# Turning cached keys: loads in 32-by-32 blocks and VectorE's block transpose in place of TensorE transposes

## Chip, cores, metric

The kernel runs on one core of a Trainium2 chip. The metric is the device time of one execution in microseconds (us); lower is better. One core has TensorE (PE: matrix products and transposes), VectorE (DVE), ScalarE (ACT), GpSimd (POOL), the SyncE queue (SP) from which this kernel issues all its DMAs, and 16 DMA engines. Each engine works through its own instructions in the order in which the compiled program has them.

## What is computed

One step of a two-layer encoder trunk for two groups of tokens: a new prompt of 512 tokens, and 8 running streams of 16 tokens each, with 256 cached rows per stream. Both groups share the weights and most of the work runs on all 640 rows at once. Cut to what matters here:

```python
for i in range(2):
    h = rmsnorm(x, g_mix[i])
    x = x + (fox_mixer(h, fox_cache) if i == 0 else mla_mixer(h, mla_cache))
    x = x + cross_attn(rmsnorm(x, g_cross[i]), mem_k[i], mem_v[i])
    x = x + swiglu(rmsnorm(x, g_ffn[i]))

# fox_mixer: 16 heads of 64; running streams see 256 cached keys and 16 new ones
s = einsum('bqhd,bkhd->bhqk', q, k_all) * FOX_SCALE + decay_bias
# cross_attn: 4 heads of 256 over 256 memory rows
s = einsum('bqhd,bkhd->bhqk', h @ w_q, mem_k) * X_SCALE
o = einsum('bhqk,bkhd->bqhd', softmax(s), mem_v) @ w_o
```

TensorE contracts over the partition axis. In `q . k` that axis is the head dimension, while the cached and memory keys lie in memory as rows of one token each. So every key tile has to be turned, from token-by-channel to channel-by-token, before its scores can be made.

## The kernel before

The program runs five kinds of stages: the FoX mixer (`fox_phase`), cross attention of layer 0 (`cross_phase`), feed-forward, the MLA mixer, cross attention of layer 1, feed-forward. Big products take weights in units of 128x1024 (`split_unit`): a DMA into one of two `raw` buffers, a rounded copy `whi` on ACT (L144), and the rest `wlo` by a subtraction on DVE (L145), with three buffers each. A product (`gemm`) is three passes over these parts, gathered in PSUM. Attention is written as lists of small steps, and `merge` spreads two or three lists evenly side by side, so that projections for the next heads stand between the steps of attention. The program's order on each engine follows from these lists; waits are on buffers and on data.

Keys are turned in three places.

- **FoX, running streams** (`sample_list` in `fox_phase`): 8 head pairs, each with two batches of 4 streams. `load` brings 128 channels of 1024 cached rows into `kr` (one buffer, 512 KB, L631), `vr` with the values, and `keys(0)`, `keys(1)` turn half of it each: four 128x128 transposes on TensorE into a PSUM tile (L641), then one copy to `KT`, on DVE for the first half (L645) and on ACT for the second (L647). That makes 32 steps.
- **Cross attention, running streams** (`sample_list` in `cross_phase`): per layer 2 head pairs x 2 batches x 2 heads x 4 streams. `keys` issues the DMA for one stream and head (256 KB, L886, ring `kr` of four buffers, shared with others), four transposes (L890), one copy (DVE L894 or ACT L896, by turns). 64 steps over both layers. `scores(0)` needs the first four of a list, `scores(1)` the other four.
- **Cross attention, prompt** (`prompt_list`): per layer 4 heads; keys and values of the prompt's memory come from DRAM (`kvd`, L827), four transposes (L835), then a split in two parts. 8 steps.

In each layer's cross attention the lists are run in four merges: the first two have the running streams, the prompt and a query projection (`q_list`) side by side, the last two have output projections in place of the query projection. `q_list` loads its 256 weight columns as two units of 128 columns with all 1024 rows, the second of them in the middle of the list:

```python
for half in range(2):
    for dt in range(2):
        if half == 0:
            L.append(lambda dt=dt: load(dt))
        L += gemm(... ws_ops(d[dt], slice(0, P), nx.T, ...), HALF, ..., parts=3)
```

Of the kernel before, what the change touches and what calls it, by code (L numbers as in the profile page):

```python
# [18 lines left out]
P = 128  # L19
# [61 lines left out]
def fox_mla_kernel(ctx: ExitStack, tc: tile.TileContext, I, O):  # L81
# [105 lines left out]
    def gemm(ops, n, done, parts=1):  # L187
        """One PSUM accumulation as a list of steps; ops() is asked for when the first step runs."""
# [15 lines left out]
    def merge(*lists):  # L204
        """Emits lists of steps side by side, each spread evenly over the whole."""
        steps = [((i + 0.5) / len(l), n, i) for n, l in enumerate(lists) for i in range(len(l))]
        for _, n, i in sorted(steps):
            lists[n][i]()
# [36 lines left out]
    class Act:  # L245
        """A transposed activation in two tiles of four row blocks each."""
# [36 lines left out]
    def out_norm(out_tile, g_row, cls=None):  # L283
        """Runs the last output projection of a phase tile by tile, each tile's norm behind it."""
# [42 lines left out]
    # ---------------------------------------------------------------- memory keys and values  # L327
    kvd = [drp.tile([2, NMEM, D], F32, name=f"kvd{l}") for l in range(2)]

    def mem_list(l, pool):  # L330
        """K and V of the prompt's memory, to the outputs and to DRAM for the cross attention."""
# [39 lines left out]
    # ---------------------------------------------------------------- FOX  # L371
    def fox_phase():
        w_in = I["w_fox_in"][0]
        w_out = I["w_fox_out"][0]
        ck = I["cache_fox_k"][0].rearrange("b (tt t) h d -> t (b tt) (h d)", t=P)
# [5 lines left out]
        with ExitStack() as st:  # L381
# [242 lines left out]
            def sample_list(pr):  # L624
# [4 lines left out]
                def load(bq):  # L629
                    d["kr"] = fp.tile([P, 8, P], F32, tag="kr", name="kr", bufs=1)  # L630
                    S.dma_start(d["kr"], ck[:, 8 * bq:8 * bq + 8, pr * P:(pr + 1) * P])  # L631
# [6 lines left out]
                def keys(b2):  # L638
                    pt = psum_t()
                    for i in range(4):  # L640
                        T.transpose(out=pt[:, i * P:(i + 1) * P], in_=d["kr"][:, 4 * b2 + i, :], identity=ident)  # L641
                    src = pt[:, :].rearrange("p (b t) -> p b t", t=PAST)
                    dst = d["KT"][:, 2 * b2:2 * b2 + 2, 0:PAST]
                    if b2 == 0:
                        V.tensor_copy(dst, src)  # L645
                    else:
                        A.copy(dst, src)  # L647
# [124 lines left out]
    # ---------------------------------------------------------------- cross attention  # L772
    def cross_phase(l, nx, rest):
        w_q, w_o = I["w_x_q"][l], I["w_x_o"][l]
        mk = I["cache_mem_k"][l].rearrange("b (m p) h d -> p (b m) (h d)", p=P)
        mv = I["cache_mem_v"][l].rearrange("b (m p) h d -> p (b m) (h d)", p=P)
        with tc.tile_pool(name=f"x{l}", bufs=2, reuse_waits="tile") as xp:
# [5 lines left out]
            def q_list(h):  # L783
# [4 lines left out]
                def load(dt):  # L788
                    if dt == 0:
                        qs_[h] = [xp.tile([P, 2, NP], F32R, tag=f"qT{i}", name=f"qT{i}", bufs=2) for i in range(2)]  # L790
                    c0 = h * XD + dt * P
                    d[dt] = load_w([(0, P, w_q[:, c0:c0 + P])], per=8)
# [11 lines left out]
                for half in range(2):  # L804
                    for dt in range(2):
                        if half == 0:
                            L.append(lambda dt=dt: load(dt))
                        L += gemm(lambda dt=dt, half=half: ws_ops(d[dt], slice(0, P), nx.T,
                                                                  slice(half * HALF, (half + 1) * HALF), KD),
                                  HALF, lambda ps, dt=dt, half=half: done(ps, dt, half), parts=3)  # L810
                return L
# [8 lines left out]
            def prompt_list(h):  # L820
                d = {}

                def load():
                    d["kv"] = []
                    for i in range(2):
                        r = xp.tile([P, 2, XD], F32, tag="kr", name="kr", bufs=4)
                        S.dma_start(r, kvd[l][i].rearrange("(t p) n -> p t n", p=P)[:, :, h * XD:(h + 1) * XD])  # L827
                        d["kv"].append(r)

                def keys():  # L830
                    d["kT"] = [xp.tile([P, 2, NMEM], F32R, tag=f"kT{i}", name=f"kT{i}", bufs=1) for i in range(2)]
                    pt = psum_t()
                    for dt in range(2):
                        for mt in range(2):
                            T.transpose(out=pt[:, dt * NMEM + mt * P:dt * NMEM + (mt + 1) * P],  # L835
                                        in_=d["kv"][0][:, mt, dt * P:(dt + 1) * P], identity=ident)
                    evac_split(d["kT"][0], d["kT"][1], pt.rearrange("p (d m) -> p d m", m=NMEM))
                    d["v"] = [xp.tile([P, 2, XD], F32R, tag=f"v{i}", name=f"v{i}", bufs=1) for i in range(2)]
                    evac_split(d["v"][0], d["v"][1], d["kv"][1])
# [37 lines left out]
            def sample_list(pr, bq):  # L877
# [3 lines left out]
                def keys(hh, b):  # L881
                    hc = slice((2 * pr + hh) * XD, (2 * pr + hh + 1) * XD)
                    if b % 2 == 0:
                        d["KT"][b // 2] = xp.tile([P, 2, 2, NMEM], F32, tag="KT", name="KT", bufs=2)
                    kr = xp.tile([P, 2, XD], F32, tag="kr", name="kr", bufs=4)
                    S.dma_start(kr, mk[:, 2 * (4 * bq + b):2 * (4 * bq + b) + 2, hc])  # L886
                    pt = psum_t()
                    for dt in range(2):
                        for mt in range(2):
                            T.transpose(out=pt[:, dt * NMEM + mt * P:dt * NMEM + (mt + 1) * P],  # L890
# [807 lines left out]
```

## Time and profile before

| | |
|---|---|
| median of 3 runs | 2170.16 us (2169.56 to 2170.47) |
| the profiled execution, first to last instruction | 2169.7 us |
| instructions in it | 36108 |
| TensorE busy / VectorE / ScalarE / GpSimd | 98% / 65% / 42% / 8% of the span |
| TensorE clock granted, mean | 0.997 of full speed |
| DMA | 234.34 MB, mean 108 GB/s |

The profiled execution's span stands for its own time; the median of the runs is 0.5 us above it. A busy share says how long an engine had an instruction in flight; a matmul is pipelined with the next, so what one costs is read from the distance between starts, not from its duration.

### The profile page before, as it was taken

Reading aid. Unit: us, or ns where it says so; the run is one execution under the profiler, and the core shown is the slowest. Engines: PE = TensorE matmul, PEld = TensorE weight load, DVE = VectorE, ACT = ScalarE, POOL = GpSimd, SP = SyncE. Lnnn points to the kernel's source line nnn. Section 1 sums busy time; section 2 is a strip of 40 time slices with the busy share of each in tenths; the row PEclk is TensorE's granted clock in tenths of the full one; section 3 lists DMA queues with packets and bytes.
Section 4 is the critical chain, followed back from the end, with each engine's and each line's share of the span. In section 5 each row is a group of like instructions: output and inputs, shape, how many; then the busy total and the mean of one; then the engine's idle time right before and its main releaser. Section 6 shows DMA issues by size and latency. Waiting matters only on the chain. (4 is left out here: it accounts for less than half of the span.)

```text
span 2169.7 us, 36108 instructions
## 1 busy us (share of the span) xinstructions
PE 2116.0 (98%) x14253; PEld 1862.4 (86%) x14253; DVE 1404.2 (65%) x2719; ACT 904.0 (42%) x1809; POOL 178.7 (8%) x354
## 2 busy tenths in 40 slices
PE   7999999999999999999999999999999999999998
PEld 7888888888977799999999877777886799999997
DVE  5455555655446796687676566667545796786685
ACT  4444434554433453343334454544433443343342
POOL 1222121120000000000000200100100000000000
PEclk9999999999999999999999999999999999999999
DMA  8353443576354322222221320112435322322221
GB/s 235 112 145 107 127 124 116 178 231 211 108 178 143 117 78 79 87 88 78 78 78 53 109 72 26 51 40 60 154 129 190 94 84 78 98 75 82 78 88 59
DMA packets 279273, 234.34 MB, mean 108 GB/s; under 512 B 15664, under 2 KB 255920, under 8 KB 279104
## 3 DMA queue, kind: packets, MB, share of 16 engines
q1 hardware_dynamic: 279104, 232.03, 34.9%
q8 instruction: 113, 1.85, 0.4%
q14 instruction: 56, 0.46, 0.1%
HBM read 214.79 MB, written 17.21 MB: 107 GB/s over the span
## 5 line engine op out<-in xcount | busy, mean ns | idle before, releaser
L198 PE MATMUL mm<-hT,whi 128*128 128x320 f32 x1744 | 296.3, 314 | 3.3 <-ACT hT L216 3.3
L198 PEld LDWEIGHTS mm<-hT,whi 128*128 128x128 f32 x1744 | 261.1, 188 | 16.0 <-issue 9.8
L312 DVE TENSOR_TENSOR X<-mm,X 128x512 f32<-128x512 f32 x270 | 183.2, 687 | 127.5 <-PE mm L198 125.6
L145 DVE TENSOR_TENSOR wlo<-raw,whi 128x1024 fp32r<-128x1024 f32 (+4 forms) x145 | 169.7, 1175 | 105.8 <-ACT whi L144 69.8
L144 ACT CAST whi<-raw 128x1024 fp32r<-128x1024 f32 (+4 forms) x145 | 144.0, 1002 | 122.7 <-PE mm L198 75.6
L198 PE MATMUL mm<-whi,oT 128*128 128x512 f32 x544 | 185.2, 413 | 2.4 <-DVE X L312 2.1
L1069 ACT CAST whi<-tw 128x512 fp32r<-128x512 f32 (+1 forms) x120 | 91.9, 766 | 213.8 <-PE mm L198 127.5
L198 PE MATMUL mm<-whi,aT 128*128 128x512 f32 x560 | 173.0, 390 | 0.3 <-ACT aT L1034 0.3
L198 PE MATMUL mm<-hT,wlo 128*128 128x320 f32 x872 | 157.4, 313 | 0.0
L198 PEld LDWEIGHTS mm<-hT,wlo 128*128 128x128 f32 x872 | 133.7, 188 | 3.6 <-issue 3.5
L198 PE MATMUL mm<-whi,hT 128*128 128x256 f32 (+2 forms) x800 | 126.8, 297 | 1.9 <-ACT hT L216 1.0
L198 PE MATMUL mm<-s,whi 128*128 128x320 f32 x768 | 128.2, 309 | 0.0
L226 POOL TENSOR_SCALAR rstd<-ss 128x1 f32<-128x1 f32 x49 | 16.7, 340 | 1306.2 <-ACT hn L224 1302.1
L198 PEld LDWEIGHTS mm<-whi,aT 128*128 128x128 f32 x560 | 104.4, 188 | 22.5 <-ACT aT L1034 1.2
L198 PEld LDWEIGHTS mm<-whi,oT 128*128 128x128 f32 x544 | 98.0, 190 | 26.1 <-issue 5.7
L198 PEld LDWEIGHTS mm<-s,whi 128*128 128x128 f32 x768 | 116.6, 188 | 0.0
L198 PEld LDWEIGHTS mm<-whi,hT 128*128 128x128 f32 x800 | 109.5, 192 | 7.8 <-issue 3.2
L1070 DVE TENSOR_TENSOR wlo<-tw,whi 128x512 fp32r<-128x512 f32 (+1 forms) x120 | 103.4, 862 | 19.0 <-ACT whi L1069 18.3
L198 PE MATMUL mm<-wlo,oT 128*128 128x512 f32 x272 | 109.9, 406 | 0.0
L198 PE MATMUL mm<-wlo,aT 128*128 128x512 f32 x280 | 108.8, 389 | 0.0
L212 PE MATMUL ps_s<-kT,qT 128*128 128x256 f32 (+8 forms) x576 | 102.5, 329 | 0.2 <-ACT qs L1503 0.2
L1069 ACT CAST whi<-raw 128x1024 fp32r<-128x1024 f32 x44 | 46.3, 1052 | 131.7 <-PE mm L198 71.4
(337 smaller groups left out, 4342.6 us busy)
## 6 DMA issues: line engine op xcount, KB each, us to landing
rawg<-w_ffn_gu SPq DMA_DIRECT2D x80, 512.0 KB, 3.8
raw<-w_ffn_down SPq DMA_DIRECT2D x44, 512.0 KB, 3.6
raw<-w_x_kv SPq DMA_DIRECT2D x32, 512.0 KB, 4.8
kr<-cache_mem_k SPq DMA_DIRECT2D x64, 256.0 KB, 4.2
vr<-cache_mem_v SPq DMA_DIRECT2D x32, 512.0 KB, 4.6
raw<-w_fox_in SPq DMA_DIRECT2D x30, 512.0 KB, 4.3
kr<-cache_fox_k SPq DMA_DIRECT2D x16, 512.0 KB, 5.5
vr<-cache_fox_v SPq DMA_DIRECT2D x16, 512.0 KB, 3.9
```

Source lines behind the costliest of these rows:

```text
L144: A.copy(hi[:, 0:m], raw[:, 0:m])
L145: V.tensor_tensor(lo[:, 0:m], raw[:, 0:m], hi[:, 0:m].bitcast(F32), ALU.subtract)
L198: T.matmul(st["ps"][:, 0:n], lhsT=l, rhs=r, start=(j == 0), stop=(j == m - 1))
L212: T.matmul(out, lhsT=la[li], rhs=ra[ri], start=start and i == 0, stop=stop and i == 2)
L226: G.tensor_scalar(r, ss, EPS, None, ALU.add)
L312: V.tensor_tensor(xs, ps, xs, ALU.add)
L1069: A.copy(hi[:, o:o + m], src)
L1070: V.tensor_tensor(lo[:, o:o + m], src, hi[:, o:o + m].bitcast(F32), ALU.subtract)
```

## The change

Keys are no longer loaded as whole rows. A load brings 32 rows (`j`) of every 32-row block onto 32 partitions, 32 (FoX) or 64 (cross) channels wide, in four DMAs, one for each quarter of the partitions. VectorE's block transpose, which turns every 32x32 block in place, then writes the key tile channel-by-token straight to SBUF. TensorE, PSUM and the copies on DVE or ACT are no longer used for it. In cross attention a 64-channel block is turned as two interleaved 32-channel blocks, so that channel `2p + t` lands on partition `p` of half `t`; the query weights follow, read with a step of two columns, and are loaded as two units of 512 rows and 256 columns, both at the head of the list. `kr` has two buffers instead of one in FoX and six instead of four in cross attention, where the prompt's turned keys (`ktp`) take one too. The scratch for software-made DMAs is cut to 1024.

```diff
-        ck = I["cache_fox_k"][0].rearrange("b (tt t) h d -> t (b tt) (h d)", t=P)
+        ck = I["cache_fox_k"][0].rearrange("b (m j) h d -> j (b m) (h d)", j=32)
...
                 def load(bq):
-                    d["kr"] = fp.tile([P, 8, P], F32, tag="kr", name="kr", bufs=1)
-                    S.dma_start(d["kr"], ck[:, 8 * bq:8 * bq + 8, pr * P:(pr + 1) * P])
+                    d["kr"] = fp.tile([P, 32, 32], F32, tag="kr", name="kr", bufs=2)
+                    for i in range(4):
+                        c0 = pr * P + 32 * i
+                        S.dma_start(d["kr"][32 * i:32 * i + 32], ck[:, 32 * bq:32 * bq + 32, c0:c0 + 32])
...
                 def keys(b2):
-                    pt = psum_t()
-                    for i in range(4):
-                        T.transpose(out=pt[:, i * P:(i + 1) * P], in_=d["kr"][:, 4 * b2 + i, :], identity=ident)
-                    src = pt[:, :].rearrange("p (b t) -> p b t", t=PAST)
-                    dst = d["KT"][:, 2 * b2:2 * b2 + 2, 0:PAST]
-                    if b2 == 0:
-                        V.tensor_copy(dst, src)
-                    else:
-                        A.copy(dst, src)
+                    V.transpose(d["KT"][:, 2 * b2:2 * b2 + 2, 0:PAST],
+                                d["kr"][:, 16 * b2:16 * b2 + 16, :].rearrange("p (b m) i -> p b (m i)", b=2))
...
-        mk = I["cache_mem_k"][l].rearrange("b (m p) h d -> p (b m) (h d)", p=P)
+        mk = I["cache_mem_k"][l].rearrange("b (m j) h d -> b j m (h d)", j=32)
...
-                def load(dt):
-                    if dt == 0:
-                        qs_[h] = [xp.tile([P, 2, NP], F32R, tag=f"qT{i}", name=f"qT{i}", bufs=2) for i in range(2)]
-                    c0 = h * XD + dt * P
-                    d[dt] = load_w([(0, P, w_q[:, c0:c0 + P])], per=8)
+                def load():
+                    qs_[h] = [xp.tile([P, 2, NP], F32R, tag=f"qT{i}", name=f"qT{i}", bufs=2) for i in range(2)]
+                    d["w"] = load_w([(0, XD, w_q[:, h * XD:(h + 1) * XD])])
+
+                def ops(dt, half):
+                    hs = slice(half * HALF, (half + 1) * HALF)
+                    return [(d["w"].get(wi, k).rearrange("p (n t) -> p t n", t=2)[:, dt], nx.T[ai][:, k, hs])
+                            for wi, ai in PASSES for k in range(KD)]
...
+                        L += gemm(lambda dt=dt, half=half: ops(dt, half), HALF,
+                                  lambda ps, dt=dt, half=half: done(ps, dt, half), parts=3)
+                return [load] + L
+
+            def load_keys(src, h):
+
+                r = xp.tile([P, 8, 64], F32, tag="kr", name="kr", bufs=6)
+                for g in range(4):
+                    c0 = h * XD + 64 * g
+                    S.dma_start(r[32 * g:32 * g + 32], src[:, :, c0:c0 + 64])
+                return r
+
+            def turn_keys(dst, r):
+                V.transpose(dst, r.rearrange("p m (i t) -> p t m i", t=2))
...
+                    d["k"] = load_keys(kvd[l][0].rearrange("(m j) n -> j m n", j=32), h)
+                    d["vr"] = xp.tile([P, 2, XD], F32, tag="kr", name="vp", bufs=6)
...
-                    evac_split(d["kT"][0], d["kT"][1], pt.rearrange("p (d m) -> p d m", m=NMEM))
+                    kt = xp.tile([P, 2, NMEM], F32, tag="kr", name="ktp", bufs=6)
+                    turn_keys(kt, d["k"])
+                    evac_split(d["kT"][0], d["kT"][1], kt)
...
-                    kr = xp.tile([P, 2, XD], F32, tag="kr", name="kr", bufs=4)
-                    S.dma_start(kr, mk[:, 2 * (4 * bq + b):2 * (4 * bq + b) + 2, hc])
-                    pt = psum_t()
-                    for dt in range(2):
-                        for mt in range(2):
-                            T.transpose(out=pt[:, dt * NMEM + mt * P:dt * NMEM + (mt + 1) * P],
-                                        in_=kr[:, mt, dt * P:(dt + 1) * P], identity=ident)
-                    src = pt.rearrange("p (d m) -> p d m", m=NMEM)
-                    if b % 2 == 0:
-                        V.tensor_copy(d["KT"][b // 2][:, 0], src)
-                    else:
-                        A.copy(d["KT"][b // 2][:, 1], src)
+                    turn_keys(d["KT"][b // 2][:, b % 2], load_keys(mk[4 * bq + b], 2 * pr + hh))
...
-            for f in ql[:6] + rest[:1] + ql[6:8] + rest[1:] + ql[8:] + q_list(1):
+            for f in ql[:5] + rest[:1] + ql[5:7] + rest[1:] + ql[7:] + q_list(1):
...
-    nc = bacc.Bacc("TRN2", target_bir_lowering=False, num_devices=1)
+    nc = bacc.Bacc("TRN2", target_bir_lowering=False, num_devices=1, dynamic_dma_scratch_size=1024)
```

## Rows read from the trace of the kernel before

**Rows 1.** The page: engines' busy us, share, instructions; a weight unit's subtraction.

```profile
PE 2116.0 (98%) x14253; PEld 1862.4 (86%) x14253; DVE 1404.2 (65%) x2719; ACT 904.0 (42%) x1809; POOL 178.7 (8%) x354
...
L145 DVE TENSOR_TENSOR wlo<-raw,whi 128x1024 fp32r<-128x1024 f32 (+4 forms) x145 | 169.7, 1175 | 105.8 <-ACT whi L144 69.8
```

**Rows 2.** Stages: from:to, length, busy us of five engines, PE clock, DMA share, GB/s.

```profile
60.00:492.00 432.00, 429.12 (x3542) 376.16 (x3542) 241.37 (x633) 195.63 (x428) 94.18 (x173) 1.00 0.48 143
577.00:710.00 133.00, 126.65 (x935) 100.48 (x933) 71.17 (x142) 49.53 (x113) 0.00 (x0) 0.99 0.48 155
1564.00:1700.00 136.00, 128.72 (x958) 102.26 (x957) 71.87 (x143) 50.20 (x115) 0.00 (x0) 1.00 0.47 155
```

**Rows 3.** Tile `kr`: TensorE's weight loads for the three kinds of transposes, min/median/max ns.

```profile
L890 PEld LDWEIGHTS ps_t<-cst,kr x256: 137/141/231, 576.7 to 1685.5; 128*128 128x128 f32 x128
L641 PEld LDWEIGHTS ps_t<-cst,kr x128: 137/140/143, 70.2 to 492.3; 128*128 128x128 f32 x128
L835 PEld LDWEIGHTS ps_t<-cst,kr x32: 138/140/146, 580.4 to 1676.0; 128*128 128x128 f32 x32
```

**Rows 4.** Timeline of weight loads, cross attention: start us, length, engine, instruction.

```profile
580.36 0.50 PEld L835 LDWEIGHTS ps_t<-cst,kr 128*128 128x128 f32 x4
580.83 0.47 PEld L890 LDWEIGHTS ps_t<-cst,kr 128*128 128x128 f32 x4
581.27 0.30 PEld L198 LDWEIGHTS mm<-hT,wlo 128*128 128x128 f32 x2
```

**Rows 5.** Tile `KT`: a small weight load, and the copies out of PSUM.

```profile
L662 PEld LDWEIGHTS ps_s<-KT,Qbd x128: 106/108/109, 78.1 to 497.7; 128*32 128x32 f32 x128
L896 ACT COPY KT<-ps_t x32: 586/587/593, 577.9 to 1686.0; 128x512 f32<-128x512 f32 x32
L894 DVE COPY KT<-ps_t x32: 677/692/693, 578.5 to 1684.2; 128x512 f32<-128x512 f32 x32
...
L645 DVE COPY KT<-ps_t x16: 670/680/692, 71.0 to 489.0; 128x512 f32<-128x512 f32 x16
L647 ACT COPY KT<-ps_t x16: 581/587/587, 74.9 to 492.7; 128x512 f32<-128x512 f32 x16
```

**Rows 6.** DMA issues: count, KB of each, median us from issue to landing.

```profile
kr<-cache_mem_k SPq DMA_DIRECT2D x64, 256.0 KB, 4.2
...
kr<-cache_fox_k SPq DMA_DIRECT2D x16, 512.0 KB, 5.5
...
pw<-cache_fox_logf SPq DMA_DIRECT2D x2, 64.0 KB, 3.7
```

**Rows 7.** SP's queue in FoX: the second load of cached keys.

```profile
74.85 0.38 SPq L631 DMA_DIRECT2D kr<-cache_fox_k  x1
```

**Rows 8.** Weight loads in FoX: the first transposes of that load.

```profile
92.18 0.42 PEld L641 LDWEIGHTS ps_t<-cst,kr 128*128 128x128 f32 x4
```

**Rows 9.** One stretch late in FoX, columns as in rows 2.

```profile
420.00:480.00 60.00, 58.64 (x520) 53.49 (x520) 33.21 (x68) 31.67 (x62) 12.46 (x19) 1.00 0.79 241
```

**Rows 10.** More stretches: one FoX key load alone, a merge's head and its remainder.

```profile
122.50:127.00 4.50, 4.50 (x41) 4.50 (x39) 0.76 (x2) 1.82 (x4) 1.65 (x4) 1.00 0.41 117
...
642.70:656.50 13.80, 12.47 (x74) 9.70 (x70) 7.72 (x13) 3.56 (x8) 0.00 (x0) 1.00 0.87 283
656.50:676.00 19.50, 19.50 (x144) 13.86 (x143) 11.65 (x26) 8.60 (x19) 0.00 (x0) 1.00 0.21 70
```

**Rows 11.** TensorE's timeline at a merge's head: transposes that waited for their keys.

```profile
619.43 0.63 PE L890 MATMUL ps_t<-cst,kr 128*128 128x128 f32 x4 [2.14 <-DMA kr<-cache_mem_k]
```

**Rows 12.** SP's queue ahead of layer 0's merges: the first load of memory keys.

```profile
530.94 0.57 SPq L886 DMA_DIRECT2D kr<-cache_mem_k  x1
```

**Rows 13.** Weight loads of a query projection, 128 columns each.

```profile
559.12 2.39 PEld L198 LDWEIGHTS mm<-hT,whi 128*128 128x128 f32 x16
561.47 0.19 PEld L198 LDWEIGHTS mm<-hT,wlo 128*128 128x128 f32 x1
```

More of the change, by code (lines that the diff above doesn't have):

```diff
@@ L805, in q_list @@
                     for dt in range(2):
[L806 to L811, printed above, removed]
+                        L += gemm(lambda dt=dt, half=half: ops(dt, half), HALF,
[9 more added lines that the diff above has]
+                V.transpose(dst, r.rearrange("p m (i t) -> p t m i", t=2))
             def softmax(pw, sp):
@@ L823, in load @@
                 def load():
[L824 to L828, printed above, removed]
+                    d["k"] = load_keys(kvd[l][0].rearrange("(m j) n -> j m n", j=32), h)
+                    d["vr"] = xp.tile([P, 2, XD], F32, tag="kr", name="vp", bufs=6)
+                    S.dma_start(d["vr"], kvd[l][1].rearrange("(t p) n -> p t n", p=P)[:, :, h * XD:(h + 1) * XD])
                 def keys():
                     d["kT"] = [xp.tile([P, 2, NMEM], F32R, tag=f"kT{i}", name=f"kT{i}", bufs=1) for i in range(2)]
-                    pt = psum_t()
-                    for dt in range(2):
-                        for mt in range(2):
-                            T.transpose(out=pt[:, dt * NMEM + mt * P:dt * NMEM + (mt + 1) * P],
-                                        in_=d["kv"][0][:, mt, dt * P:(dt + 1) * P], identity=ident)
-                    evac_split(d["kT"][0], d["kT"][1], pt.rearrange("p (d m) -> p d m", m=NMEM))
+                    kt = xp.tile([P, 2, NMEM], F32, tag="kr", name="ktp", bufs=6)
+                    turn_keys(kt, d["k"])
+                    evac_split(d["kT"][0], d["kT"][1], kt)
                     d["v"] = [xp.tile([P, 2, XD], F32R, tag=f"v{i}", name=f"v{i}", bufs=1) for i in range(2)]
-                    evac_split(d["v"][0], d["v"][1], d["kv"][1])
+                    evac_split(d["v"][0], d["v"][1], d["vr"])
                     oTp[h] = [xp.tile([P, 2, NP], F32R, tag=f"oT{i}", name=f"oT{i}", bufs=3) for i in range(2)]
@@ L881, in keys @@
                 def keys(hh, b):
-                    hc = slice((2 * pr + hh) * XD, (2 * pr + hh + 1) * XD)
                     if b % 2 == 0:
                         d["KT"][b // 2] = xp.tile([P, 2, 2, NMEM], F32, tag="KT", name="KT", bufs=2)
-                    kr = xp.tile([P, 2, XD], F32, tag="kr", name="kr", bufs=4)
-                    S.dma_start(kr, mk[:, 2 * (4 * bq + b):2 * (4 * bq + b) + 2, hc])
[L887 to L890, printed above, removed]
-                                        in_=kr[:, mt, dt * P:(dt + 1) * P], identity=ident)
-                    src = pt.rearrange("p (d m) -> p d m", m=NMEM)
-                    if b % 2 == 0:
-                        V.tensor_copy(d["KT"][b // 2][:, 0], src)
-                    else:
-                        A.copy(d["KT"][b // 2][:, 1], src)
+                    turn_keys(d["KT"][b // 2][:, b % 2], load_keys(mk[4 * bq + b], 2 * pr + hh))
                 def scores(hh):
@@ L932, in values @@
                     if hh == 1:
-                        d["osb"] = xp.tile([P, 512], F32, tag="kr", name="osb", bufs=4)
+                        d["osb"] = xp.tile([P, 512], F32, tag="kr", name="osb", bufs=6)
                         A.copy(d["osb"], d["op"])
```

## Prediction

> **What bounds the kernel now.** I read the page first. TensorE is busy for 98% of the span, VectorE for 65%, ScalarE for 42% [rows 1]. An average can hide a stage with another limit, so I looked at the stretches in which keys are turned: FoX with its running streams, and the four merges of cross attention in either layer [rows 2]. In FoX TensorE is busy for 429.1 of 432 us, in the merges for 126.7 of 133 and 128.7 of 136, at full clock. VectorE has 56%, 54% and 53% there, ScalarE 45% and less. So TensorE's queue sets the pace, and its time is worth its full price wherever nothing else ends a wait later. The merges have about 6 to 7 us each time in which TensorE is idle; who ends that is looked at below.
>
> **What is removed.** The tile view counts the transposes: 256 and 32 in cross attention, 128 in FoX [rows 3]. A transpose lasts longer in the trace than it costs, since it overlaps the next; the price is the distance between starts. A step of four begins at 580.36, the next step at 580.83, the product behind it at 581.27 [rows 4]: 0.47 and 0.44 us, so 0.46 a step. FoX has 32 steps: 14.7 us. Each of the eight merges has 8 steps of the streams and 1 of the prompt: 72 steps, 33.1 us. All of it is 47.8 us, 2.2% of the span, and it is the most that the removal by itself can give.
>
> With it go the copies, 32 + 16 on VectorE and 32 + 16 on ScalarE, 0.69 and 0.59 us each [rows 5]. ScalarE gets 28 us back, which is worth nothing while it is busy for under half of these stages [rows 2].
>
> **What is added on VectorE.** A block transpose of 128x512 is in no row. Below, it can't cost nothing; the nearest row is the copy of the same 512 elements, 0.69 us [rows 5]; above I take the 128x1024 subtraction, 1.18 us [rows 1]. I use 0.69. Then 48 transposes stand for 48 copies, and 56 are new on VectorE (48 that ScalarE copied, 8 of the prompt): 39 us, five of them in each merge, 3.4 us of some 33. VectorE goes from 54% to about 64% there; at 1.18 us (9 x 1.18 - 4 x 0.69 = 7.9 us) to 78%. The cover is VectorE's idle time, and it holds at both ends.
>
> In cross attention the transpose reads every second word, which no row shows. [...]
>
> **What is added on the DMA side.** One FoX key load alone on the queue, 1024 runs of 512 bytes, makes the 16 engines 41% busy for 4.5 us: 1.85 us of all of them [rows 10]. Afterwards it is 4096 runs of 128 bytes. If bytes alone count it still costs 1.85; if each run costs what a 512-byte run costs, 7.4. A row leans to the cheap side: the forget values come as 1024 runs of 64 bytes and land after 3.7 us, the 512-byte runs after 5.5 [rows 6]. I take the middle, 4.6. Sixteen loads then add 44 us of DMA to 432 us that are 48% busy: 58%. A load's last part is issued three issues of 0.38 us later [rows 7], and four quarters one behind the other would land after some 9 us, at worst 4 x 3.7 = 15. The shortest time of the sixteen from issue to first transpose is 17.3 us (74.85 to 92.18) [rows 7, 8], and with two buffers the issue only moves forward. So in FoX the wait that moves from TensorE to VectorE is normally over before VectorE comes to it. Only late in FoX is the DMA crowded, 79% [rows 9]; there I give 2 us back. **FoX: -12.7 us** (ends: -14.7; and -8, if 7 of the 22 us that the last four loads add at most turn into waits).
>
> In the merges it is tighter. A merge's first 13.8 us run the DMA at 87% and 283 GB/s, and then it falls to 21% [rows 10]: the loads that waited for buffers start together. TensorE feels it: its transposes waited 2.14 us for keys there [rows 11]. At 283/0.87 = 325 GB/s a 256 KB key load costs 0.81 us of the 16 engines; as 1024 runs of 256 bytes between 0.81 and 1.85, and I take 1.3. Before the first scores of a merge stand four key loads and the prompt's: 2.5 us more of a DMA that is nearly full (ends: 0 and 5.2). The three extra issues for each load, 0.37 us each, hide behind that. Against it stands that TensorE no longer waits for each key tile but goes on with projections, and that the six buffers let more loads start at once. What is late next is `scores(0)`, which needs four turned tiles. A transpose that waits holds VectorE's queue: the subtractions of weights, the residual adds and the softmax sums behind it, and TensorE then waits for these. I take a loss of 2 us for each of the six merges that begin behind another one; the first of each layer has its keys early (issued from 530.9 on, first turned at 576.7 [rows 3, 12]) and loses nothing. **Merges: 6 x (-4.1 + 2) + 2 x -4.1 = -20.8 us** (ends: -33.1, and -2 when each head loses 5.2).
>
> **The moved query weights.** Both units now stand ahead of the list's first product, and that product needs both. The second cast on ScalarE comes earlier by one unit's time, and the third buffer of `whi` and `wlo` is taken by the next list while the previous one still reads. I price that with one unit's 1.18 us [rows 1] for two of the four lists in each layer, covered for the others by the other lists' products: up to 4.7 us, of which I take **+2**. Their loads have longer runs now, a small gain that I leave out.
>
> **The query weights' step of two.** The stationary operand is now read with every second column, 4 heads x 4 products x 24 x 2 layers = 768 weight loads. Now 16 of them start within 2.39 us, 147 ns apart (2.39 - 0.19 over 15) [rows 13]. A load of 32 columns takes 108 ns [rows 5], one of 128 takes 190 [rows 13]: 0.85 ns a column, so 128 stream in about 109 ns and hide behind a product of 147. If the step costs nothing, nothing changes; if it halves the rate, 218 ns stick out by 71 each, 55 us. No row has such a load. I take nothing, since a load can grow by 38 ns, a third, before it shows.
>
> [...]
>
> The smaller scratch and the PSUM tiles set free cost nothing and cover nothing that a row shows to be short.
>
> **The sum.** 2169.7 - 12.7 - 20.8 + 2 = 2138.2 us for the profiled execution; with the 0.5 us by which the median of the runs lies above it, 2138.7, said as 2139.
>
> **The rivals.**
> *Everything comes back, and waits too.* All 47.8 us, perhaps also the waits for keys at the heads, some 1 us each in eight merges: 2122 down to 2114. For it speaks TensorE at 98%; against it the crowded heads.
> *Late keys eat the gain of cross attention.* Heads lose 5.2 us each, VectorE's queue stands still behind a transpose, and only FoX and the first merges gain: -12.7 - 2 + 2, about 2157. For it: 87% DMA. Against it: the 21% behind each head, into which late loads can move.
> *The stepped weight load halves its rate* (slower, one mechanism): 2139 + 55 = 2194. It decides the sign from 31.5 us / 768 = 41 ns more between products, a distance of 188 ns. A smaller growth would land between, so I count from 2160 on as this case.
> *Short runs cost more than long ones.* If a 256-byte run costs twice a 512-byte one, a key load takes 3.7 us of all engines, nine of them 33 us, and the rest of a merge's DMA about 9 (48% of 33 us less nine loads of 0.81): 42 us in a merge of 33, so 9 x 8 = 72 us lost against FoX's gain: about 2230. It decides from about 3 us a load. Against it: 64-byte runs landed no later than 512-byte ones [rows 6].
> [...]
> *No change:* the transposes stood in time that TensorE had to spare. FoX at 99% busy speaks against it.
>
> **How the numbers follow.** Chances: the forecast, 2125 to 2153, 0.50; everything back 0.13; late keys, 2153 to 2166, 0.17; no change 0.05; stepped load 0.10; short runs 0.05. I forecast 2139. A range of 2112 to 2171 leaves out most of the two slow cases and a little below: about 2 in 10. A measurement of this kernel tells a difference from about 0.2%, 4.3 us. Faster by more: 0.50 + 0.13 + most of 0.17 = 0.79; within: 0.06; slower: 0.15.
>
> **What would show it.** In the profile after: no TensorE rows on `kr`; VectorE's block transposes near 0.69 us; FoX shorter by 12 to 15 us with VectorE rarely idle for key loads; the merges shorter by 15 to 30 us in all, with waits of VectorE on key loads at the heads; the query projections' products still 147 ns apart. The prediction is wrong if these are 180 ns apart or more, if the block transpose takes over 2 us, if key loads take over 10 us to land in the merges, or if VectorE's waits at the heads last longer than the transposes did.

## The result, and the profile after

The changed kernel takes 2198.89 us (median of 4 runs, 2196.23 to 2202.58) against 2169.95 for the kernel before on the same chip (4 runs): ratio 1.0141, interval 1.0125 to 1.0156. The forecast was 2139, with a range up to 2171. The change costs 29 us where 31 us of gain were forecast. The ratios, here and below, leave out one run of the experiment e2, which took 2257 us at a granted clock of 0.85.

I read the page first. These are the busy times of the engines and the DMA issues that answer to [rows 1, 6].

```profile
PE 2107.3 (96%) x13837; PEld 1832.4 (84%) x13837; DVE 1435.8 (65%) x2775; ACT 875.3 (40%) x1761; POOL 177.3 (8%) x354
...
kr<-cache_mem_k SPq DMA_DIRECT2D x256, 64.0 KB, 2.3
...
kr<-cache_fox_k SPq DMA_DIRECT2D x64, 128.0 KB, 5.5
```

TensorE is busy for 8.7 us less, in a span that is 24.7 us longer: it now waits. The next question is where. FoX is told by the last turn of its outputs, first in the kernel before, then in the changed one (timeline of TensorE):

```profile
511.11 0.33 PE L694 MATMUL ps_t<-cst,osb 128*128 128x128 f32 x1
```

```profile
498.16 0.33 PE L689 MATMUL ps_t<-cst,osb 128*128 128x128 f32 x1
```

FoX ends 12.9 us earlier; 12.7 were forecast. The loss lies in cross attention. Here are both layers of it in the kernel before, from the first product of the query projection to the first of the feed-forward; the columns are those of [rows 2].

```profile
548.80:750.80 202.00, 193.79 (x1339) 160.94 (x1338) 112.30 (x199) 75.46 (x157) 5.33 (x12) 0.99 0.45 142
1536.70:1733.70 197.00, 187.86 (x1311) 156.17 (x1310) 108.63 (x195) 74.45 (x156) 4.05 (x9) 1.00 0.43 137
```

The same in the changed kernel, with FoX ahead (first row), then the second and the fourth merge of layer 0 and one stretch in which key loads are issued without a gap:

```profile
60.00:492.00 432.00, 428.90 (x3516) 373.65 (x3515) 254.41 (x664) 193.53 (x427) 91.28 (x175) 1.00 0.60 155
...
534.10:757.80 223.70, 196.70 (x1195) 153.28 (x1194) 123.59 (x218) 65.84 (x142) 5.49 (x12) 0.95 0.48 134
1543.40:1758.50 215.10, 188.99 (x1169) 146.73 (x1169) 119.98 (x215) 65.38 (x141) 4.29 (x9) 0.97 0.49 133
...
596.90:637.90 41.00, 35.29 (x219) 26.35 (x218) 20.13 (x41) 11.24 (x28) 0.00 (x0) 0.88 0.54 150
688.40:729.00 40.60, 27.88 (x153) 17.39 (x152) 17.20 (x36) 7.59 (x20) 0.00 (x0) 0.85 0.43 113
...
598.00:613.00 15.00, 13.37 (x85) 11.74 (x84) 7.10 (x16) 3.22 (x8) 0.00 (x0) 0.93 0.58 135
```

In FoX TensorE is busy for 428.9 of 432 us as before, and the DMA share rose to 0.60 (0.58 was forecast). Cross attention is longer by 21.7 and 18.1 us, although its transposes are gone. TensorE is idle for 53.1 us of these two stretches, where it was 17.4; and it is busy for 385.7 us, where it was 381.7 with some 33 us of transposes in it. So half of the loss is idle time, and the other half is that the work left to TensorE lasts longer, in part at a lower clock (0.95 and 0.97 in place of 0.99 and 1.00). Merges two and four take 41 us each; TensorE is idle for 5.7 and 12.7 us of them, and its granted clock falls to 0.88 and 0.85, means over stretches at 1.00 (598 to 606) and at 0.50 (626 to 628, 726 to 730). That last row matters most: in the head of a merge, where the kernel before had 87% and 283 GB/s [rows 10], the DMA engines are now busy for 58% and move 135 GB/s. They aren't full.

SyncE's queue shows why (timeline, one merge's key loads and then its first value loads):

```profile
590.37 2.38 SPq L813 DMA_DIRECT2D kr<-cache_mem_k  x4
592.79 4.66 SPq L813 DMA_DIRECT2D kr<-kvd  x4
...
597.99 14.98 SPq L813 DMA_DIRECT2D kr<-cache_mem_k  x28
613.02 1.01 SPq L913 DMA_DIRECT2D vr<-cache_mem_v  x2
```

SyncE issues 28 DMAs in 14.98 us, 0.53 us each, back to back, and a merge's 36 key DMAs take it 22 us; some 3 us of these are waits between the four loads from `kvd` (4.66 us). For the 14.98 us the queue has no gap, while the DMA engines are busy for 58%: I take it that the issuing sets the pace there, not the moving.

What TensorE waited for, answering to [rows 11] (us in total, times, longest):

```profile
PE ps_o L917 <- DMA vr<-cache_mem_v: 10.1, 7, 2.6
PE ps_s L892 <- DVE KT L817: 9.7, 8, 2.0
...
PE ps_s L212 <- ACT pws L823: 9.0, 8, 1.1
PE ps_s L212 <- ACT kT L216: 6.5, 2, 3.2
```

And a piece of the second merge on TensorE: no projection stands between the steps of attention.

```profile
616.63 1.05 PE L892 MATMUL ps_s<-KT,Qp 128*32 128x256 f32 x10 [2.02 <-DVE KT L817]
618.09 3.47 PE L892 MATMUL ps_s<-KT,Qp 128*32 128x256 f32 x16 [0.41 <-DVE KT L817]
622.67 0.50 PE L212 MATMUL ps_s<-kT,qT 128*128 128x256 f32 x2 [1.11 <-ACT pws L823]
```

The program's order on TensorE has changed. It doesn't simply follow from the lists, as I wrote of the kernel before: the framework fixes it when the program is built, and it depends on the form of the loads, since e2 and e7 below differ in their key DMAs alone and get different orders. By what rule it orders them no run shows. Second merge, products counted (each s and v is two rows in the trace): Q, O projections; k turning of streams' or prompt's keys; S, T, V scores, transposes, values of the prompt; s, t, v, u those of the streams and the turn of their outputs.

```
before Q8 k4 Q13 k4 Q2 k8 Q5 S2 Q3 k4 S10 k4 Q1 s8 T4 Q3 k4 V1 Q3 k4 V11 k4 Q5 s8 Q8 S12 t2 Q8 T1 Q2 v8 Q4 T3 Q17 ...
after  Q52 S12 s2 T1 S5 T3 S1 V9 s1 V3 s13 S6 t2 T1 Q8 T3 v8 Q21 ...
e2     Q25 S2 Q11 S10 Q4 s8 T4 Q4 s1 V1 s1 S4 V11 s6 S2 Q7 S6 Q1 t2 Q8 T1 v1 T3 v7 Q21 ...
```

In the changed kernel 52 projection products stand in a block ahead and attention follows without cover.

The operations themselves cost what was forecast. VectorE's turns (mean ns behind the comma) and the weight loads of a query projection, read with a step of two:

```profile
L817 DVE STREAM_TRANSPOSE KT<-kr 128x512 f32<-128x512 f32 x64 | 42.5, 691 | 6.1 <-PE ps_s L892 6.1
L641 DVE STREAM_TRANSPOSE KT<-kr 128x512 f32<-128x512 f32 x32 | 21.7, 694 | 0.0
L817 DVE STREAM_TRANSPOSE ktp<-kr 128x512 f32<-128x512 f32 x8 | 5.6, 703 | 0.0
```

```profile
555.04 2.40 PEld L198 LDWEIGHTS mm<-hT,whi 128*128 128x128 f32 x16
```

### The profile page after: what moved, and what is told of

Read it like the earlier page. It is cut to its first block, busy times and chain, and to the rows that moved or that the text cites. A ratio compares the mean times of both kernels' runs of the same rounds, so it can differ in the third digit from the quotient of the medians.

```text
span 2194.4 us, 35580 instructions
## 1 busy us (share of the span) xinstructions
PE 2107.3 (96%) x13837; PEld 1832.4 (84%) x13837; DVE 1435.8 (65%) x2775; ACT 875.3 (40%) x1761; POOL 177.3 (8%) x354
## 5 line engine op out<-in xcount | busy, mean ns | idle before, releaser
L198 PE MATMUL mm<-whi,oT 128*128 128x512 f32 x544 | 179.8, 407 | 2.6 <-DVE X L312 1.8
L212 PE MATMUL ps_s<-kT,qT 128*128 128x256 f32 (+8 forms) x576 | 108.5, 336 | 16.4 <-ACT pws L823 9.0
L212 PEld LDWEIGHTS ps_s<-kT,qT 64*128 64x128 f32 (+2 forms) x576 | 73.3, 192 | 37.8 <-ACT pws L823 13.0
```

Of the source, the lines that this page charges most:

```text
L198: T.matmul(st["ps"][:, 0:n], lhsT=l, rhs=r, start=(j == 0), stop=(j == m - 1))
L212: T.matmul(out, lhsT=la[li], rhs=ra[ri], start=start and i == 0, stop=stop and i == 2)
```

## Experiments

Theories, as the expectations name them: **Q**, the query weights cost it. **O** and **P**, the order on TensorE. **L**, **S**, **B**, the keys come late: in general, by the number of issues on SyncE, because all are issued from a merge's boundary on (**B2**: behind value loads in the queue). **R**, runs of 256 bytes are too dear in themselves. **N**, number and place of issues.

The table has every run, and from each profiled execution the change against before by stage: FoX to its last turn, cross attention of layer 0 up to the first feed-forward product on sums, cross attention of layer 1 likewise. The stages between changed by 2.2 us at most, in e1 by 4.9.

| run | us | ratio to before (interval) | FoX | cross 0 | cross 1 |
|---|---|---|---|---|---|
| after | 2198.9 | 1.0141 (1.0125-1.0156) | -12.9 | +19.9 | +18.7 |
| e1 | 2161.9 | 0.9952 (0.9933-0.9970) | -5.8 | -4.9 | -3.7 |
| e2 | 2130.5 | 0.9811 (0.9792-0.9830) | -10.7 | -18.1 | -14.2 |
| e3 | 2229.2 | 1.0268 (1.0250-1.0286) | -6.3 | +33.2 | +31.6 |
| e4 | 2170.4 | 0.9999 (0.9988-1.0010) | +1.8 | -2.8 | +3.3 |
| e5 | 2188.7 | 1.0085 (1.0070-1.0100) | -11.0 | +15.3 | +14.5 |
| e6 | 2220.0 | 1.0232 (1.0211-1.0252) | -9.3 | +26.6 | +28.6 |
| e7 | 2181.3 | 1.0054 (1.0035-1.0072) | -9.8 | +9.2 | +10.4 |
| e8 | 2213.5 | 1.0203 (1.0184-1.0222) | -9.9 | +28.0 | +27.8 |
| e9 | 2207.7 | 1.0180 (1.0157-1.0203) | -10.9 | +19.5 | +27.0 |
| e10 | 2211.7 | 1.0193 (1.0170-1.0217) | -10.2 | +27.4 | +26.9 |
| e11 | 2209.8 | 1.0186 (1.0167-1.0204) | -9.2 | +23.2 | +22.9 |
| e12 | 2200.6 | 1.0140 (1.0121-1.0158) | -11.3 | +16.8 | +24.3 |
| e13 | 2192.5 | 1.0111 (1.0090-1.0131) | -10.4 | +15.6 | +16.4 |
| e14 | 2161.1 | 0.9958 (0.9943-0.9973) | -9.4 | -5.1 | +3.3 |
| e15 | 2279.1 | 1.0514 (1.0497-1.0532) | -9.2 | +59.3 | +57.0 |
| e16 | 2206.3 | 1.0178 (1.0163-1.0193) | -10.5 | +24.4 | +23.1 |
| e17 | 2153.3 | 0.9932 (0.9915-0.9948) | -8.9 | -6.1 | -4.6 |
| e18 | 2169.9 | 1.0008 (0.9999-1.0018) | -11.7 | +4.5 | +3.5 |

**e1, FoX alone.** `cross_phase` as before, `fox_phase` as changed:

```diff
-        mk = I["cache_mem_k"][l].rearrange("b (m j) h d -> b j m (h d)", j=32)
+        mk = I["cache_mem_k"][l].rearrange("b (m p) h d -> p (b m) (h d)", p=P)
```

> The change in FoX alone; cross attention turns its keys on TensorE as before. In the trace of the changed kernel FoX ends 12.9 us earlier than before (last turn of outputs at 498.2 against 511.1), and both cross attentions lose about 20 us each. If the parts don't act on one another, this kernel takes 2170.0 - 12.9 = 2157 us (2153 to 2161), under all theories. If FoX's new loads also delay what comes behind them (weights, memory keys of the first merge), 2160 to 2170.

2161.9, in the range for loads that also delay what comes behind them; 0.48% is 10.4 us. In its profiled execution FoX is 5.8 us shorter, cross attention, whose code is as before, 8.6, and the stages between are 4.9 longer. So FoX gains by itself, but the same FoX code gave 5.8 us here and 12.9 in the changed kernel, and no run shows why.

**e2, whole rows.**

```diff
-                for g in range(4):
-                    S.dma_start(r[32 * g:32 * g + 32], src[:, :, c0:c0 + 64])
+                S.dma_start(r.rearrange("p (t n) c -> p t (n c)", t=2), src[:, :, h * XD:(h + 1) * XD])
```

> The changed kernel, but in cross attention the keys come as whole rows in one DMA each, as before, and VectorE turns these; the keys that are multiplied are then not the reference's. The program's order on TensorE is again one with projections between the steps of attention. Theory O (in the changed kernel the order of the program on TensorE puts the projections ahead and leaves attention without cover; the framework chose it at build time): 2125 to 2145, below the FoX part alone. Theory L (keys in short runs really land late on the chip): the same, since the runs are long. Theory Q (the query weights' step of two, or their two units at the head of the list, cost the 36 us that each layer lost): stays at 2190 to 2200.

2130.5. Cross attention now gains 18.1 + 14.2 = 32.3 us, nearly all of the 33.1 that the transposes cost. Everything of the change but the key DMAs and the order that goes with them is still there, so these 68 us belong to them; theory Q falls. SyncE's queue at the same place, the window of it, and what one issue takes in e2 and in the changed kernel (min/median/max ns):

```profile
592.00 0.43 SPq L810 DMA_DIRECT2D kr<-cache_mem_k  x1
592.47 0.47 SPq L810 DMA_DIRECT2D kr<-kvd  x1
...
593.49 9.34 SPq L810 DMA_DIRECT2D kr<-cache_mem_k  x7
```

```profile
592.00:602.90 10.90, 10.32 (x77) 9.09 (x76) 4.96 (x10) 2.75 (x6) 0.00 (x0) 1.00 0.83 274
```

```profile
L810 SPq DMA_DIRECT2D kr<-cache_mem_k x64: 367/368/1089, 519.7 to 1637.7; - x64
```

```profile
L813 SPq DMA_DIRECT2D kr<-cache_mem_k x256: 311/449/1688, 517.0 to 1710.6; - x128
```

Nine key tiles in 10.8 us at 83% of the DMA, where the changed kernel needs 22 us. An issue of 256 KB takes SyncE no longer than one of 64 KB does there; nine of them at the median of 0.37 us make 3.3 of the 10.8 us. The rest SyncE waits; that it waits for buffers wasn't shown.

**e3, the order of the code.**

```diff
+    def matmul(self, *a, **k):
+        i = nc.tensor.matmul(*a, **k)
+        return tc.keep_in_program_order(i) if pinned[0] else i
```

> The changed kernel with its own short-run loads, its block transposes and its weights, but in the four merges of each layer TensorE's instructions keep the order of the code, so that projections stand between the steps of attention. Theory O: the loss goes, 2125 to 2150. Theory L: TensorE now stands in line behind each late key tile, so 2195 or more. Theory Q: 2190 to 2200.

2229.2: worse, as theory L had it. Theory O falls in this form: under these loads the block order is the lesser evil.

**e4, the query projection alone,** in the kernel before:

```diff
-                    d[dt] = load_w([(0, P, w_q[:, c0:c0 + P])], per=8)
+                    d["w"] = load_w([(0, XD, w_q[:, h * XD:(h + 1) * XD])])
...
+                    return [(d["w"].get(wi, k).rearrange("p (n t) -> p t n", t=2)[:, dt], nx.T[ai][:, k, hs])
```

> The kernel before with the changed query projection alone: weights read with a step of two columns and both units at the head of the list; keys are loaded and turned on TensorE as before, so the channels of queries and keys don't pair as in the reference. By the prediction's terms +2 (0 to 4.7) and 0 for the step: 2170 to 2175. Theory Q: 2190 or more. Theory O: 2165 to 2176, since the order of the program hardly changes.

No difference that can be measured.

**e5 and e6, orders exchanged.** TensorE's instructions of the merges are chained in a given order, that of the changed kernel (e5, on e2) or that of e2 (e6, on the changed kernel).

```diff
+        for w in text.split():                 # "F24 S12 F3 ...", counts by kind
+            for _ in range(int(w[1:])):
+                i = rec[w[0]].pop(0)
+                if prev is not None:
+                    tc.add_manual_dep(i, prev.name, NoSync, reason="order")
+                prev = i
```

> The kernel of e2 (whole rows, one DMA a key tile, turned on VectorE; keys not the reference's), but in the four merges of each layer TensorE's instructions are put into exactly the order that they have in the changed kernel. Theory P (it is the order on TensorE that costs; the loads themselves do no harm on the chip): 2165 to 2200. Theory S (SyncE's queue: each key tile is four DMAs, each takes SyncE about half a us to issue, 36 key DMAs a merge take 18 us, and whatever order TensorE has, keys and values behind them come late): the order alone costs little, 2130 to 2150.

> The changed kernel with its four short-run DMAs for each key tile, but with TensorE's instructions in the merges in exactly the order that they have in e2, which took 2130.5 us. Theory P: 2130 to 2150. Theory S: slow for all that, 2190 to 2235, since keys and values are issued late, as in e3.

e5: 2188.7, so the block order alone costs 58 us under fast loads; that is more than theory S allowed. e6: 2220.0, so the good order doesn't help under the slow loads, against P. For the gain, fast loads and e2's order are both needed: the two forms of load differ by 10 us under the block order (2198.9 against 2188.7) and by 90 under e2's (2220.0 against 2130.5). In e5 TensorE is idle for 4.1 of 44 us from 596 to 640 in layer 0's cross attention; in the changed kernel it is 5.7 of 41 (596.9 to 637.9). In e6 28 key DMAs took SyncE just as long as in the changed kernel, and TensorE waited for turned keys:

```profile
603.84 14.87 SPq L851 DMA_DIRECT2D kr<-cache_mem_k  x28
```

```profile
PE ps_s L93 <- DVE KT L855: 28.9, 19, 2.0
PE ps_s L93 <- ACT kT L254: 20.9, 6, 3.9
```

**e7, whole rows in four DMAs.**

```diff
-                S.dma_start(r.rearrange("p (t n) c -> p t (n c)", t=2), src[:, :, h * XD:(h + 1) * XD])
+                for g in range(4):
+                    S.dma_start(r[32 * g:32 * g + 32].rearrange("p (t n) c -> p t (n c)", t=2),
+                                src[32 * g:32 * g + 32, :, h * XD:(h + 1) * XD])
```

> The kernel of e2, but each key tile of cross attention is loaded by four DMAs of 32 rows of tokens each, so the bytes, the runs of 1 KB and the turned data are those of e2, and only the number of DMAs is that of the changed kernel (keys not the reference's). Theory S (number of DMAs on SyncE's queue): 2180 to 2205. Theory R (runs of 256 bytes cost the DMA engines too much): 2130 to 2140.

2181.3, in S's range and far from R's: 51 of the 68 us come with the number of the DMAs, in runs of 1 KB. The rest, 17.6 us, comes with the short runs. The framework's order is nearly that of the changed kernel (`Q52 S12 s2 T1 S5 ...` in the second merge). That order would account for the 51 us by itself: e5 has it with one DMA a tile, and takes 2188.7. What four DMAs in runs of 1 KB cost on the chip under e2's order was not run; with the short runs e6 shows it. SyncE, and a window over the same 28 issues:

```profile
598.86 14.37 SPq L811 DMA_DIRECT2D kr<-cache_mem_k  x28
```

```profile
598.90:613.20 14.30, 13.11 (x93) 10.85 (x91) 7.95 (x16) 3.56 (x9) 0.00 (x0) 1.00 0.50 142
```

0.51 us an issue with 64 runs each, 0.53 with 256: in this size the issue costs by the DMA and hardly by the run, and half of the DMA engines' time is free.

**e8, four streams in a DMA.**

```diff
+                            S.dma_start(d["ks"][32 * g:32 * g + 32], mk[:, m0:m0 + 32, c0:c0 + 64])
```

> The changed kernel, but the keys of four streams and one head come in four DMAs (one for each quarter of the partitions, 256 KB each) instead of sixteen; the runs are still 256 bytes and the result is that of the reference. Such a load has two buffers of its own. Theory S: 12 + 4 DMAs for keys less a merge save 12 us or so of SyncE's time, so most of the loss goes: 2135 to 2165. Theory R: 2190 to 2205.

2213.5, a miss for S and above R's range too. Issues of 256 KB took 1.1 us each in the median (min/median/max ns below), the DMA share there was 1.26 (above 1, so packets that overlap in time are added up), and a first key tile waits for 1 MB in two buffers; TensorE waited 25.5 us for values that stood behind.

```profile
L890 SPq DMA_DIRECT2D ks<-cache_mem_k x64: 317/1113/3275, 519.3 to 1709.8; - x64
```

```profile
602.40:609.90 7.50, 5.51 (x24) 5.11 (x23) 4.33 (x8) 3.01 (x5) 0.00 (x0) 0.50 1.26 197
```

**e9, e10, e11, half of the issues elsewhere, more buffers,** all in e6's order. (From e10 on the pool of one-column tiles grew with the key ring; in e18 it didn't.)

```diff
-                    S.dma_start(r[32 * g:32 * g + 32], src[:, :, c0:c0 + 64])
+                    (S, A)[g % 2].dma_start(r[32 * g:32 * g + 32], src[:, :, c0:c0 + 64])
...
-                        v = xp.tile([P, 4, XD], F32, tag="vr", name="vr", bufs=2)
+                        v = xp.tile([P, 4, XD], F32, tag="vr", name="vr", bufs=4)
```

> The kernel of e6 (four short-run DMAs a key tile, TensorE in the order of e2, 2220 us), but two of the four DMAs of each key tile are issued from ScalarE's queue; bytes, runs and buffers are the same, and the result is that of the reference. Theory S (issuing on SyncE's one queue): 18 issues of half a us leave SyncE in each merge, 9 us of some 45, and most of the loss goes: 2135 to 2185. Theory R (runs of 256 bytes are too dear for the DMA engines): nothing changes, 2205 to 2225.

> The kernel of e6, but with four buffers for the streams' values instead of two and eight for keys instead of six, so that SyncE doesn't stand behind a value load that waits for its buffer, and the next merge's keys can be issued earlier; all DMAs stay on SyncE. Theory S in its first form (36 key issues a merge simply take too long): little gain, 2195 to 2220. Theory S in its second form (the queue stands behind value loads, and the issues come all at once after that): 2135 to 2170. Theory R: 2205 to 2225.

> e9 and e10 together: half of the key DMAs on ScalarE's queue, four buffers for values, eight for keys, TensorE in the order of e2. Theory S in either form: close to e2, 2125 to 2150, with the reference's result. Theory R: 2195 to 2225.

2207.7, 2211.7, 2209.8: 8 to 12 us of the 90 between e6 and e2. S missed in e9 and e11, and in e10 in its second form, while the ranges for R (and for S in its first form, in e10) held. The rows of e11 show what ScalarE's queue did: ScalarE's half is issued between its own casts, the last one of this merge at 625.53, when SyncE's half had been out since 611.7, and VectorE waited for these keys.

```profile
606.26 1.36 ACTq L851 DMA_DIRECT2D kr<-cache_mem_k  x3
613.41 0.32 ACTq L851 DMA_DIRECT2D kr<-cache_mem_k  x1
615.72 3.57 ACTq L851 DMA_DIRECT2D kr<-cache_mem_k  x5
625.53 0.32 ACTq L851 DMA_DIRECT2D kr<-cache_mem_k  x1
```

```profile
  DMA kr<-cache_mem_k: 32.5, 23
```

**e12, e13, e14, keys issued a merge early.** The prompt's key load and the first 6 (4) of a merge's 8 stream loads become steps in the second half of the merge before; e13 has three value buffers too.

```diff
+            for h in range(4):
+                merge(sl[h][1], pl[h][1], fill[h], [lambda: None] * 4 + pre[h + 1])
```

> The changed kernel with its four short-run DMAs a key tile, all on SyncE, but the prompt's keys and the first six of a merge's eight stream key tiles are issued during the merge before (code order; eleven key buffers instead of six); the result is that of the reference, and TensorE's order is what the framework makes of it. Theory B (a merge's 36 key DMAs are issued only from its boundary on and take 20 us there, twice as long as nine whole-row DMAs, so that the second scores of every merge come 10 us later): spread over the merge before, they are hidden, 2130 to 2160. Theory R (runs of 256 bytes are too dear wherever they stand): 2190 to 2215.

> As e12 with the first four of the eight stream key tiles and the prompt's issued early, ten key buffers and three for values. Theory B: the first scores have their keys, the second ones still depend on 16 DMAs issued in the merge, so between e12 and the changed kernel: 2140 to 2175. Theory R: 2190 to 2215.

> e12 with two of the four DMAs of each key tile on ScalarE's queue. Theory B: SyncE needs 9 us less a merge, so as e12 or a little better, 2125 to 2155; if ScalarE's own work suffers, up to 2165. Theory R: 2190 to 2215.

2200.6, 2192.5 and 2161.1, all in the framework's own order: against the changed kernel early loads on SyncE alone change -6 to +2 us, inside R's range, and together with the second queue they gain 38, far outside it. So 256-byte runs in four DMAs a tile are not too dear in themselves (R falls). B's ranges were missed by e12 and e13. The second queue without early loads was not run in the framework's own order. In e12 the early loads didn't come early enough: after 572.5 SyncE issued nothing until 598.68, then two value loads, and the keys behind them from 600.76 on. That the value load waited for its buffer is my reading; in the changed kernel SyncE's value loads waited 100.1 us in all for TensorE's products that read the values before, 19.9 the longest.

```profile
570.57 1.93 SPq L813 DMA_DIRECT2D kr<-cache_mem_k  x4
598.68 0.94 SPq L918 DMA_DIRECT2D vr<-cache_mem_v  x2
```

**e15, e16, e17, the value loads out of the way.** e15 is e12, e16 is e14, each with the edit below; e17 is e14 with `bufs=3` for `vr` and five early loads.

```diff
-                        S.dma_start(v, mv[:, 8 * bq + 4 * b2:8 * bq + 4 * b2 + 4, hc])
+                        G.dma_start(v, mv[:, 8 * bq + 4 * b2:8 * bq + 4 * b2 + 4, hc])
```

> e12 (all key DMAs on SyncE, six of eight issued a merge early; 2200 us), but the streams' value loads, which wait for their two buffers, are issued from GpSimd's queue, where nothing else waits in these merges. In e12 SyncE stood 26 us behind such a value load (572.5 to 598.7) and issued the keys after it. Theory B2 (the time is lost because the keys stand behind value loads in the one in-order queue, and four DMAs a tile are too slow to catch up after it): SyncE goes on issuing, 2135 to 2165. Theory R (short runs too dear in themselves): 2190 or more.

> e14 (half of the key DMAs on ScalarE's queue, six of eight issued early; 2161 us) with the value loads on GpSimd's queue. Theory B2: both ways out together, 2130 to 2155, below the FoX part alone. If value loads from GpSimd are dear themselves, about 2160 or more.

> e14 with three value buffers in place of two and one key buffer less (five of eight stream tiles early); values stay on SyncE. Theory B2: SyncE stands behind values for a shorter time, 2140 to 2160.

e15 and e16 tell nothing of B2, since they made a new wait: in e15 GpSimd sent the value loads of a merge one at a time, 4.2 to 5.4 us apart, each of the later ones after a load had landed or TensorE had gone on, and TensorE waited 57.1 us for values. e16 sends them the same way.

```profile
603.72 0.83 POOL L918 DMA_DIRECT2D vr<-cache_mem_v  x1 [61.43 <-PE ps_o L922]
608.73 0.76 POOL L918 DMA_DIRECT2D vr<-cache_mem_v  x1 [4.18 <-DMA vr<-cache_mem_v]
```

e17 is the fastest of the kernels whose keys are the reference's: 2153.3, 0.9932 of before, below both kernels. From e1 the intervals don't part it. The range for B2 held, but with a value buffer more and an early load fewer at once, so B2 isn't shown.

**e18, two streams in a DMA, early, on two queues.**

```diff
+                        (S, A)[g % 2].dma_start(r[32 * g:32 * g + 32], mk[:, m0:m0 + 16, c0:c0 + 64])
```

> The changed kernel with short runs of 256 bytes throughout, but the keys of two streams come in four DMAs of 128 KB (20 key DMAs a merge instead of 36), two of each four on ScalarE's queue, and three of a merge's four pairs and the prompt's keys are issued during the merge before; two value buffers as in the changed kernel, and the result is that of the reference. Theory N (the number and place of the issues binds, not the runs): fewer issues than in e14 (2161) and e17 (2153), 2130 to 2152. Theory R (runs too dear): no better than those, 2153 to 2165.

2169.9: N misses, and so does R. Fewer issues didn't help; values came late again (31.6 us, against 18.3 in e14 and, with three value buffers, 15.6 in e17).

```profile
PE ps_o L926 <- DMA vr<-cache_mem_v: 31.6, 12, 4.6
```

## Why the prediction was wrong, step by step

- *TensorE sets the pace; the transposes are worth 14.7 and 33.1 us.* Right: FoX gave 12.9, and cross attention gave 32.3 once its keys came as whole rows (e2).
- *A block transpose takes 0.69 us, and VectorE hides it.* Right: 0.69 and 0.70. The step of two words doesn't show: 691 ns with it, 694 without.
- *FoX: -12.7.* Right in sign and size: -12.9 in the changed kernel, DMA share 0.60 against 0.58. That it is so close is luck, since the other profiles of the same FoX code gave 5.8 to 11.7. VectorE was never idle before a FoX turn (0.0 in its row): the slack of 17 us and more [rows 7, 8] hid the longer issuing.
- *Moved query weights +2, the step of two 0.* Right within what e4 can tell (0.9999, some 2.5 us either way). The loads still start 147 ns apart, (2.40 - 0.19) / 15, as in [rows 13]; the rival of 55 us falls.
- *Merges: -20.8.* **Wrong, and here the prediction failed**, in two sentences. "The three extra issues for each load, 0.37 us each, hide behind that": they didn't hide. I priced a key load in time of the 16 DMA engines, and there I was on the dear side (1.3 us; 0.58 of the time at 135 GB/s makes 1.13), and took SyncE's issuing to be covered by it. But a load is four issues of 0.53 us in a row, 2.1 us, and SyncE has one queue; at a merge's boundary, where the loads begin together, 36 of them take 22 us against 10.8 for nine whole-row loads. "I take a loss of 2 us for each of the six merges": measured over the eight merges it is 38.6 + 33.1 = 72 us, 9 a merge. By e7 51 of the 68 us between the two forms of load come with the number of the DMAs, 17.6 with the runs; how much of the 51 is SyncE's time on the chip and how much the order that such loads bring about at build time, no run parts.
- *What is late next is `scores(0)`, and VectorE's queue stands still.* Only partly. VectorE idled just 6.1 us before its turns, and that until TensorE's scores had read the old `KT`. I held the order of the program for fixed. It is remade at build time: with these loads the projections went ahead in blocks, and the loss shows as bare attention and a clock of 0.85 to 0.88 in two merges. The order follows from the loads, and most of the loss goes through it: imposed on fast loads it costs 58 us (e5); undone under slow loads it gains nothing (e6, e3), since then TensorE stands waiting for the keys (for turned keys of the streams 28.9 us in e6 and 12.3 in e3, where 28.4 for values stand beside them).
- *Rivals.* "Late keys eat the gain" came nearest: it had keys late at the heads, for the DMA engines' time and not for SyncE's, and priced them at 5.2 us a head. "Short runs cost more than long ones" put the price on the DMA engines; they were busy 58% while SyncE issued without a gap. By engine share for each GB/s, a run of 256 bytes costs 1.2 to 1.4 times one of 1 KB (0.58/135 against 0.50/142 in e7 and 0.83/274 in e2), not a doubling; only in e8's crowded window, where the share adds up overlapping packets, it is 1.8 times e7's (1.26/197).

Open stays what parts e17 (2153) from e2 (2130). Fewer and larger DMAs (e8, e18) didn't close it, and values on GpSimd's queue couldn't be used to part B2 from the rest. I argue, but haven't shown, that it is the place of key and value loads in the queues, as in e12, where keys stood behind a value load. A rival is open: e17 runs in an order on TensorE of its own, and it wasn't run in e2's.

## What to carry to other kernels

Price a DMA twice: by the engines that move it, and by the queue that issues it, with everything that stands behind it there. Where loads begin together at a stage's boundary, the count of issues can set when the last key is there; splitting each load in four to spare TensorE 0.46 us cost SyncE some 1.8 us there (4 x 0.535 less the 0.37 of e2). Where slack of several loads stands between issue and use, as in FoX, the same change was a gain.
And when an engine's steps are taken out of a list that a framework orders, compare the order of the new program with the old one before trusting a sum made on the old.

## What the runs showed of the hardware that I hadn't expected

- Issuing a DMA of 64 KB took SyncE 0.53 us with 256 runs (changed kernel, 28 in 14.98 us) and 0.51 with 64 (e7, 28 in 14.37 us), when issued back to back; 256 KB in 256 runs took 0.37 in the median (e2), in 1024 runs 1.1 (e8; the DMA share was 1.26 where four of them stood). In the changed kernel the 16 engines were busy for 58% of the time that SyncE took to issue those 28, so issuing was the longer of the two.
- Value loads from GpSimd's queue followed one another 4.2 to 5.4 us apart within a merge (e15), with `dynamic_dma_scratch_size` at 1024; no run here sends them from there with another.
- TensorE's granted clock fell to 0.85 in the changed kernel over a merge (688.4 to 729.0) in which it was idle for 12.7 of 40.6 us.
